# An encoder layer: x read transposed, and the norm's factor moved behind the input projection

## The chip, the cores and the metric

One core of one Trainium2 chip. The metric is the time in microseconds (us) of one execution on the device; the numbers given are medians of several runs.

## The reference

One layer for two request groups that share all weights: a prompt of 2048 tokens and a sample group of 8 x 16 = 128 tokens, 1024 features each. All data are float32.

```
h   = rms_norm(x, norm_g[0])                 # x * rsqrt(mean(x*x) + 1e-6) * g, per token
z   = h @ w_in                               # 1024 -> 3592 columns
qa, ka, va, qb, kb, vb, ob, ib, fb = split(z)
att = chunk-band attention(qa, ka, va)       # 8 heads x 64, own chunk of 64 and 8 before it
hb  = mLSTM(qb, kb, vb, ib, fb)              # 4 heads x 128, matrix memory, blocks of 64
mix = concat(rms_norm(att), sigmoid(ob) * head_norm(hb)) @ w_out
x   = x + rms_norm(mix, norm_g[1])
x   = x + rms_norm(conv_ffn(rms_norm(x, norm_g[2])), norm_g[3])
```

The outputs are x of both groups, the keys and values of the last 512 prompt tokens and of the sample, and the mLSTM and convolution states. Inputs may be laid out in another order before the launch, with no arithmetic.

## The kernel before, in words

Tokens are handled in 17 tiles of 128 rows: tiles 0 to 15 are the prompt, tile 16 (`SAMPLE`) the sample group. The input projection works on two halves, each of three chunks of up to three tiles (`HALVES`): half 0 is 0-2, 3-5, 6-7 and the sample; half 1 is 8-10, 11-13, 14-15.

Each float32 factor of a large product is held as a high and a low part (`hi` rounded to float32r, `lo` the rest), and `mm3` issues three matmuls. So a chunk in SBUF is a tile `hT` [128, 2, 8, 384]: the parts, the 8 blocks of 128 features on the partitions, and the tokens. There are three such buffers (pool phT); a chunk of half 1 takes the buffer of a chunk of half 0 when its last matmul is done.

`norm_tile` (from `norm_steps`) makes one tile of a chunk: it loads the rows `xr` [128 tokens, 1024], ScalarE (ACT) squares them with a running sum, GpSimd (POOL) makes the factor per token by a power of -0.5, VectorE (DVE) multiplies the rows by the factor and by the gain row, and `rows_to_T` transposes the tile in 8 matmuls against the identity on TensorE (PE, tile `hT_pt`) and writes both parts, ACT the high one and DVE the low one.

The projection runs in 14 groups of 256 weight columns for each half, in the order va0, qk0, qk1, va1, qk2, qk3, then qb0, vo0 to qb3, vo3. `load_group` brings a group's weights in two halves through one buffer (`wraw`, tensor `wi_raw`) and splits them a group ahead. In `group_rows` (va, vo) the tokens are the output's partitions, in `group_T` (qk, qb) the features are. Each accumulates 24 matmuls in one of two PSUM buffers (`ps_mm`), evacuates to a stage tile `st` (`evac_scaled`, on ACT, with a constant scale for queries and keys), and stores it to DRAM from ACT's queue.

Attention and mLSTM run beside the projection. They are streams of small units (`att_stream`, `mem_stream`), cut by yields that state their cost on PE and DVE. After each step of a projection group `pump` adds its stated costs to a clock and starts side units only while

```
clock[1] < SHARE * clock[0]        # DVE costs against 0.615 of the PE costs
```

The steps of `load_group` and `norm_steps` are taken along as `ahead` and counted too. Half 0's tiles are made during its first group and half 1's during half 0's last group (vo3, from its third tile on) and half 1's first. `project` multiplies by w_out, two tiles ahead in its loads; when it loads tile 8 it calls `drain`, which runs what is left of the side units without regard to the clock, then closes the pool of the first phase and opens the FFN's (`open_ffn`, `h2_units`).

The final order of instructions on each engine is not that of the program. A scheduler with a model of the machine's time issues on each engine what is ready first, by program order among what is ready; `keep_in_program_order` pins an instruction behind those before it. Loads go out on SP's queue, the stores of the projection on ACT's.

Of the kernel before, what the change touches and what calls it, by code (L numbers as in the profile page):

```python
# [10 lines left out]
F32 = mybir.dt.float32  # L11
F32R = mybir.dt.float32r
# [32 lines left out]
def hymba_step(ctx: ExitStack, tc: tile.TileContext, I: dict, O: dict):  # L45
# [154 lines left out]

    def xr_tag(t):
        return "xr" if 8 <= t < SAMPLE else ("xr", "pth", "ptl")[t % 3]

    def rows_tile(tag, shape, name, dtype=F32):
# [3 lines left out]

    def norm_tile(t, chunk, j, bank):
        tag = xr_tag(t)  # L210
        xr = rows_tile(tag, [P, D], f"xr{t}")
        nc.sync.dma_start(xr, x_src(t))
        if not g0:
            g0.append(norm_row(0))
# [4 lines left out]
        nc.vector.scalar_tensor_tensor(xr, xr, rs, g0[0], op0=ALU.mult, op1=ALU.mult)  # L219
        rows_to_T(xr, chunk, j, f"hT{t}", bank)  # L220

    def evac_scaled(out, in_, scale):
        if scale is None:
            nc.scalar.copy(out, in_)
        else:
            nc.scalar.activation(out, in_, AF.Copy, scale=scale)  # L226

# [14 lines left out]
    def group_T(wh, wl, half, chunks, dsts, scales, name, outs=(None, None)):  # L242
        for c in range(2):
            for ci, tiles in enumerate(HALVES[half]):
                n = len(tiles) * P
                ch = chunks[ci]
                acc = ps_mm(f"{name}_{c}_{ci}")
                for k in range(KT):
                    w = slice(k * 256 + c * P, k * 256 + (c + 1) * P)
                    mm3(acc[:, :n], wh[:, w], wl[:, w], ch[:, 0, k, :n], ch[:, 1, k, :n],  # L250
                        start=(k == 0), stop=(k == KT - 1))
                    if k % 4 == 3:
                        yield n * 12 / 2400, 0.0
                stage = pa.tile([P, 384], F32, tag="st", name=f"{name}_st{c}_{ci}", bufs=2)
                evac_scaled(stage[:, :n], acc[:, :n], scales[c])
                store_T(stage, dsts[c], tiles, outs[c])

    def group_rows(wh, wl, half, chunks, dst, name, width=256, out=None):
        for ci, tiles in enumerate(HALVES[half]):
            for j, t in enumerate(tiles):  # L260
# [9 lines left out]
                stage = pa.tile([P, 384], F32, tag="st", name=f"{name}_st{t}", bufs=2)  # L270
                evac_scaled(stage[:, :256], acc[:, :256], None)
                if width > 256:
                    nc.vector.tensor_copy(gates[:, gate_ix(t), :], acc[:, 256:width])
                s = 4 if t == SAMPLE else t // 4
# [902 lines left out]
    g0 = []  # L1177
    pipes += [Pipe(att_stream()), Pipe(mem_stream())]
    chunks = []
    norms = norm_steps(0)  # L1180
    next(norms)
# [4 lines left out]
    for n_, (half, gi) in enumerate(seq):  # L1186
# [8 lines left out]
        if g[:2] == "va":  # L1195
            it = group_rows(wh, wl, half, chunks, vd[i], nm, 264 if gi == 0 else 256,
                            [O["v_prompt"][i], O["v_sample"][i].unsqueeze(1)])
        elif g[:2] == "qk":
            it = group_T(wh, wl, half, chunks, [qTd[i], kTd[i]], [-(DA ** -0.5), None], nm,
                         [None, [O["k_prompt"][i], O["k_sample"][i]]])  # L1200
        elif g[:2] == "qb":
            it = group_T(wh, wl, half, chunks, [[t_[:, c, :] for t_ in qkbd[i]] for c in range(2)],
                         [None, DH ** -0.5], nm)
        else:
            it = group_rows(wh, wl, half, chunks, vobd[i], nm)
        if half == 0 and gi == 13:
            chunks = []
            norms = norm_steps(1)
        if n_ == len(seq) - 1:
# [4 lines left out]
        for u, (pe, dve) in enumerate(it):  # L1214
# [374 lines left out]
def lay_inputs(inp):  # L1589
# [12 lines left out]
    for i in range(4):  # L1602
# [6 lines left out]
        "x_sample": inp["x_sample"].reshape(P, D),  # L1609
        "norm_g": inp["norm_g"][0],  # L1610
        "g_att": inp["g_att"].reshape(4, P).transpose(1, 0),
        "g_mlstm": inp["g_mlstm"],
# [66 lines left out]
```

## Time and profile before

| | us |
|---|---|
| median of 3 runs | 2814.21 |
| the runs | 2813.83 to 2818.32 |
| the profiled execution | 2812.18 |
| its span | 2810.5 |
| PE busy | 2729.8 (97%) |
| DVE busy | 1871.9 (67%) |
| ACT busy | 1407.5 (50%) |
| POOL busy | 446.2 (16%) |

Busy time is the sum over an engine's instructions, without register, semaphore and DMA-issuing ones. Matmuls overlap each other and the weight loads (PEld), so a busy PE is not PE at its peak. The projection of half 0 runs from about 12 to 531 us, that of half 1 to about 1054, the output projection to about 1330, and the FFN to the end. Names are the program's with numbers left out; L199 is line 199.

### The profile page before, as it was taken

The page shows a single profiled execution, that of the slowest core. Times are in us where ns is not written, and L with a number is a line of the kernel's source. Part 1 is how long each engine was busy: PE and PEld are TensorE (multiplying, and loading weights), DVE is VectorE, ACT ScalarE, POOL GpSimd, SP SyncE. Part 2 cuts the span into 40 slices and gives each one's busy share as a digit, 9 for nine tenths or more (in the row PEclk, how much of TensorE's full clock was granted, in tenths as well). Part 3 has the DMA queues.
Part 4 walks back from the last instruction along what each step waited for, and adds up shares of the span by engine and source line. Part 5 has one row for each costly group of instructions (what it writes and reads, how often), then busy time and mean ns, then how long its engine had stood idle before and what let it go on. Part 6 is the DMA issues. An engine that isn't in the chain of part 4 may idle for free.

```text
span 2810.5 us, 47049 instructions
## 1 busy us (share of the span) xinstructions
PE 2729.8 (97%) x16587; PEld 2550.2 (91%) x16587; DVE 1871.9 (67%) x3442; ACT 1407.5 (50%) x2836; POOL 446.2 (16%) x876
## 2 busy tenths in 40 slices
PE   8899999999999999999999999999999999999998
PEld 7899999998899998878999988799999878999887
DVE  5344455646446678666989886457878854888855
ACT  4345545644356666543545555445555543555533
POOL 1000010211100003244221110011111310222221
PEclk9999999999999999999999999999999999999999
DMA  4544355557555455355645455644544775555585
GB/s 164 170 128 125 111 155 156 177 148 215 164 173 148 141 177 172 106 180 203 199 160 173 162 177 172 218 145 154 157 154 139 266 264 155 171 181 175 188 298 197
DMA packets 313418, 486.04 MB, mean 173 GB/s; under 512 B 55426, under 2 KB 150622, under 8 KB 313054
## 3 DMA queue, kind: packets, MB, share of 16 engines
q1 hardware_dynamic: 274590, 449.21, 50.9%
q10 hardware_dynamic: 38592, 33.83, 3.6%
q8 instruction: 130, 2.13, 0.3%
q14 instruction: 106, 0.87, 0.1%
HBM read 359.36 MB, written 126.70 MB: 173 GB/s over the span
## 4 chain that ended last, share of the span: by engine, by line
PE 51%; DVE 5%; DMA 2%; issue 2%; ACT 1%; POOL 1%; SPq 0%; DVEq 0%; POOLq 0%; ACTq 0%
PE uec L95 5%; PE uec L96 5%; PE uec L97 5%; PE dn L96 4%; PE dn L97 4%; PE dn L95 4%; PE ua L97 3%; PE ua L96 3%; PE ua L95 3%; PE dnm L95 2%; PE dnm L97 2%; PE dnm L96 2%; PE wo L95 1%; PE wo L97 1%; PE wo L96 1%
## 5 line engine op out<-in xcount | busy, mean ns | idle before, releaser
L95 PE MATMUL uec<-B,wuh 128*128 128x384 f32 (+1 forms) x720 | 236.3, 329 | 6.9 <-DVE uu L1492 6.1
L96 PE MATMUL uec<-B,wuh 128*128 128x384 f32 (+1 forms) x720 | 235.2, 327 | 0.0
L97 PE MATMUL uec<-B,wul 128*128 128x384 f32 (+1 forms) x720 | 233.3, 327 | 0.0
L1251 DVE TENSOR_TENSOR gl<-gr,gh 128x768 fp32r<-128x768 f32 (+3 forms) x141 | 118.7, 849 | 163.3 <-ACT gh L1250 163.0
L1250 ACT CAST gh<-gr 128x768 fp32r<-128x768 f32 (+3 forms) x141 | 102.1, 736 | 219.1 <-PE dn L96 194.1
L1250 ACT CAST wuh<-wu 128x512 fp32r<-128x512 f32 x255 | 141.7, 617 | 91.2 <-PE uec L96 87.5
L95 PE MATMUL dn<-wdh,gh 128*128 128x512 f32 x466 | 182.9, 392 | 2.5 <-DVE ug L1403 2.5
L96 PE MATMUL dn<-wdl,gh 128*128 128x512 f32 x466 | 183.9, 395 | 0.0
L97 PE MATMUL dn<-wdh,gl 128*128 128x512 f32 x466 | 168.4, 396 | 0.0
L1251 DVE TENSOR_TENSOR wul<-wu,wuh 128x512 fp32r<-128x512 f32 x255 | 164.3, 683 | 2.8 <-DMA x2d<-mx 2.8
L96 PE MATMUL vo<-wi_l,hT 128*128 128x256 f32 x544 | 155.7, 286 | 0.0
L95 PE MATMUL vo<-wi_h,hT 128*128 128x256 f32 x544 | 154.9, 285 | 0.6 <-DVE mt L199 0.6
L97 PE MATMUL vo<-wi_h,hT 128*128 128x256 f32 x544 | 155.3, 285 | 0.0
L387 DVE CUSTOM_DVE_ANT_0 tmp<-s,nb 128x640 f32<-128x640 f32 (+4 forms) x128 | 94.3, 737 | 77.8 <-PE s L377 74.3
L95 PEld LDWEIGHTS uec<-B,wuh 128*128 128x128 f32 x720 | 135.1, 188 | 11.1 <-DVE uu L1492 8.1
L96 PEld LDWEIGHTS uec<-B,wuh 128*128 128x128 f32 x720 | 135.2, 188 | 0.1
L97 PEld LDWEIGHTS uec<-B,wul 128*128 128x128 f32 x720 | 135.0, 188 | 0.0
L388 ACT ACTIVATE tmp<-tmp,mn 128x640 f32<-128x640 f32 (+4 forms) x128 | 97.6, 762 | 69.9 <-DVE mn L387 65.6
L95 PE MATMUL qk<-hT,wi_h 128*128 128x384 f32 (+1 forms) x384 | 128.6, 335 | 3.5 <-ACT qk_st L226 1.7
L400 DVE TENSOR_TENSOR ptl<-pt,pth 128x640 fp32r<-128x640 f32 (+4 forms) x128 | 93.5, 737 | 55.4 <-ACT pth L399 54.4
L97 PE MATMUL qk<-hT,wi_l 128*128 128x384 f32 (+1 forms) x384 | 128.0, 333 | 0.0
L96 PE MATMUL qk<-hT,wi_h 128*128 128x384 f32 (+1 forms) x384 | 127.8, 333 | 0.0
(409 smaller groups left out, 8886.6 us busy)
## 6 DMA issues: line engine op xcount, KB each, us to landing
wu<-in_w_up SPq DMA_DIRECT2D x220, 256.0 KB, 4.0
wu<-wsd SPq DMA_DIRECT2D x176, 256.0 KB, 3.7
wdr<-in_w_down SPq DMA_DIRECT2D x132, 256.0 KB, 5.4
gr<-gd SPq DMA_DIRECT2D x78, 384.0 KB, 3.9
wi_raw<-in_w_in SPq DMA_DIRECT2D x52, 512.0 KB, 4.3
wsd<-ws SPq DMA_DIRECT2D x88, 256.0 KB, 4.0
gd<-g SPq DMA_DIRECT2D x44, 384.0 KB, 2.7
kraw<-kTd SPq DMA_DIRECT2D x112, 128.0 KB, 3.2
```

Of the source, the lines that this page charges most:

```text
L95: nc.tensor.matmul(out, ah, bh, start=start, stop=False, skip_group_check=onto)
L96: nc.tensor.matmul(out, ah, bl, start=False, stop=False, skip_group_check=onto)
L97: nc.tensor.matmul(out, al, bh, start=False, stop=stop, skip_group_check=onto)
L387: nc.vector.tensor_tensor_reduce(o_, s_, b_, 1.0, 3e38, ALU.add, ALU.min, accum_out=mn)
L388: nc.scalar.activation(tmp[:, :n], tmp[:, :n], AF.Exp, bias=mn, scale=-1.0, accum_out=rsum[:, i % 4, hh:hh + 1])
L400: nc.vector.tensor_tensor(s.ptl[:, sl, qc], ptv, s.pth[:, sl, qc], op=ALU.subtract)
L1250: nc.scalar.copy(h, r)
L1251: nc.vector.tensor_tensor(l, r, h, op=ALU.subtract)
```

## The change

The program gets x a second time, laid out as xT [128, 8, 2176] (feature in block, block, token), and the gain of the first norm as g0T [128, 8].

- A chunk is made from xT by `split_xT`: ACT writes the high part as x times the gain (a factor per partition), DVE the low part. There are no transposes and no multiplication by the factor per token.
- The rows are still loaded (`rows_used`) to be squared and summed; the factor of each tile goes to a column of `rsall`.
- In `group_rows` the evacuation on ACT multiplies by the factor (a scale per partition); the gates likewise on DVE.
- In `group_T`, where tokens are columns, the factor is needed along each row: `norm_factors` writes `rsall` to DRAM and reads it back to all partitions (`rsb`), and the evacuation is a DVE instruction with a constant and `rsb`. For the third chunk of half 0 it is two instructions. The step states 0.56 us of DVE for it.
- `first_half` loads pieces of xT and rows in turn through four row buffers (xr twice, pth, ptl). `second_half` loads a chunk of xT into the place of the low part and splits it there.
- For half 1 xT is first copied, DRAM to DRAM, to `xTd`, in eight DMAs that stand in the program at the fourth group of half 0 (va1, gi == 3).

```diff
+    xTd = dt_([P, KT, SEQ // 2], "xTd")
...
-        ssq = small.tile([P, 1], F32, tag="ssq", name=f"ssq{t}")
-        nc.scalar.activation(chunk[:, 0, :, j * P:(j + 1) * P], xr.rearrange("p (k c) -> p k c", k=KT), AF.Square,
-                             accum_out=ssq)
-        rs = rsqrt_mean(ssq, D, f"n0_{t}")
-        nc.vector.scalar_tensor_tensor(xr, xr, rs, g0[0], op0=ALU.mult, op1=ALU.mult)
-        rows_to_T(xr, chunk, j, f"hT{t}", bank)
...
+        def use():
+            ssq = small.tile([P, 1], F32, tag="ssq", name=f"ssq{t}")
+            nc.scalar.activation(xr, xr, AF.Square, accum_out=ssq)
+            ms = small.tile([P, 1], F32, tag="ms", name=f"n0_{t}_ms")
+            mean_square(ms, ssq, D)
+            nc.gpsimd.tensor_tensor(rsall[:, rs_ix(t):rs_ix(t) + 1], ms, nhalf[:, 0:1], op=ALU.pow)
...
+    def split_xT(ch, c, k, raw):
+        hi, lo, g = ch[:, 0, k, c], ch[:, 1, k, c], g0T[:, k:k + 1]
+        nc.scalar.activation(hi, raw, AF.Copy, scale=g)
+        nc.vector.scalar_tensor_tensor(lo, raw, g, hi, op0=ALU.mult, op1=ALU.subtract)
...
                     if k % 4 == 3:
-                        yield n * 12 / 2400, 0.0
+                        yield n * 12 / 2400, 0.0 if k < 4 else 0.56
...
-                evac_scaled(stage[:, :n], acc[:, :n], scales[c])
+                for cc, factor in rsb[half][ci]:
+                    nc.vector.scalar_tensor_tensor(stage[:, cc], acc[:, cc], scales[c], factor,
+                                                   op0=ALU.mult, op1=ALU.mult)
...
-                evac_scaled(stage[:, :256], acc[:, :256], None)
+                rs = rsall[:, rs_ix(t):rs_ix(t) + 1]
+                nc.scalar.activation(stage[:, :256], acc[:, :256], AF.Copy, scale=rs)
...
-    def norm_steps(half):
-
-        for ci, tiles in enumerate(HALVES[half]):
-            ch = phT.tile([P, 2, KT, 384], F32R, tag="hT", name=f"hT{half}_{ci}", bufs=3)
-            chunks.append(ch)
-            for j, t in enumerate(tiles):
-                norm_tile(t, ch, j, ps_big)
-                yield 0.9, 2.5
+    def norm_factors(half):
+        a, m = 9 * half, 9 - half
+        nc.sync.dma_start(rsd[a:a + m].rearrange("j p -> p j"), rsall[:, a:a + m])
+        wide = lambda j, n: rsd[j:j + n].rearrange("j p -> (j p)").unsqueeze(0).broadcast_to([P, n * P])
+        r = const.tile([P, D], F32, tag="grow", name=f"rsb{half}")
+        nc.sync.dma_start(r, wide(a, 8))
...
+    def first_half():
...
+        part(0, 0, [0], list(range(KT)))
+        for ks in ([0, 1, 2], [3, 4, 5], [6, 7]):
+            part(0, 1, [1, 2], ks)
+        for t in range(3):
+            factor(t)
+        for ci in (1, 2):
+            for i, k in enumerate(range(0, KT, 2)):
+                part(ci, 0, HALVES[0][ci], [k, k + 1])
+                if i:
+                    factor(HALVES[0][ci][i - 1])
...
+        for n in (1, 4, 3, 3, 2, 3, 3, 2):
+            go(n)
+            if not items and not loaded:
+                norm_factors(0)
+            yield 0.0, 2.2
+
+    def second_half():
+
+        for ci, tiles in enumerate(HALVES[1]):
+            ch = new_chunk(1, ci)
+            n = len(tiles) * P
+            raw = ch[:, 1].bitcast(F32)
+            nc.sync.dma_start(raw[:, :, :n], xTd[:, :, (tiles[0] - 8) * P:(tiles[0] - 8) * P + n])
+            use = rows_used(tiles[0], "xr")
+            yield 0.0, 0.0
+            use()
+            use = rows_used(tiles[1], "xr")
+            for k in range(4):
+                split_xT(ch, slice(0, n), k, raw[:, k, :n])
+            yield 0.0, 2.2
...
+            if half == 0 and gi == 3 and u < KT:
+                nc.sync.dma_start(xTd[:, u], I["xT"][:, u, SEQ // 2:SEQ])
```

More of the change, by code (lines that the diff above doesn't have):

```diff
@@ L222, in evac_scaled @@
[L222 to L226, printed above, removed]
+        def use():
[4 more added lines that the diff above has]
+            nc.gpsimd.tensor_tensor(rsall[:, rs_ix(t):rs_ix(t) + 1], ms, nhalf[:, 0:1], op=ALU.pow)
@@ new lines, in new_chunk, with part, load, factor @@
+    def new_chunk(half, ci):
+        chunks.append(phT.tile([P, 2, KT, 384], F32R, tag="hT", name=f"hT{half}_{ci}", bufs=3))
+        return chunks[-1]
+    def first_half():
+        tags = ["xr", "pth", "ptl", "xr"]
+        items = []
+        def part(ci, j, tiles, ks):
+            def load(tag):
+                ch = chunks[ci] if ci < len(chunks) else new_chunk(0, ci)
+                return staged(ch, j * P, tiles, ks, tag, f"xT{ci}_{j}_{ks[0]}")
+            items.append(load)
+        def factor(t):
+            items.append(lambda tag: rows_used(t, tag))
+        part(0, 0, [0], list(range(KT)))
[8 more added lines that the diff above has]
+                    factor(HALVES[0][ci][i - 1])
+        loaded = deque()
+        def go(n):
+            for _ in range(n):
+                while items and len(loaded) < 3:
+                    loaded.append(items.pop(0)(tags[0]))
+                    tags.append(tags.pop(0))
+                loaded.popleft()()
+        for n in (1, 4, 3, 3, 2, 3, 3, 2):
[3 more added lines that the diff above has]
+            yield 0.0, 2.2
```

56 lines of the change are left out of this document (44 added, 12 removed).

## The prediction

> **What bounds the kernel now.** I read the page's first two parts, then the busy time by windows over the first 48 us, the chain of events there in the timeline, the groups by tile, and the waits of the tensor engine.
>
> ```profile
> span 2810.5 us, 47049 instructions
> PE 2729.8 (97%) x16587; PEld 2550.2 (91%) x16587; DVE 1871.9 (67%) x3442; ACT 1407.5 (50%) x2836; POOL 446.2 (16%) x876
> ```
>
> The tensor engine (PE) is busy 97% of the span, so an instruction taken off its queue is time saved, unless it then waits for something else. All that the change touches lies in two short stretches, the start and the change of halves, and in the evacuations of the projection between them.
>
> ```profile
> 0.00:10.00 10.00, 1.83 (x8) 1.57 (x8) 2.97 (x9) 3.97 (x6) 2.64 (x17) 1.00 0.72 268
> 10.00:20.00 10.00, 7.87 (x45) 7.43 (x45) 7.67 (x9) 7.40 (x13) 2.55 (x8) 1.00 0.71 237
> 20.00:30.00 10.00, 9.87 (x85) 9.69 (x84) 8.82 (x12) 7.11 (x13) 2.94 (x5) 1.00 0.62 215
> 30.00:40.00 10.00, 10.00 (x87) 10.00 (x86) 6.67 (x10) 5.01 (x10) 0.74 (x2) 1.00 0.67 193
> sum 48.40, PE 35.78 PEld 34.45 DVE 28.22 ACT 26.66 POOL 9.60; mean PE 7.16 PEld 6.89 DVE 5.64 ACT 5.33 POOL 1.92
> ```
>
> Columns are PE, PEld, DVE, ACT, POOL, then clock, DMA share and GB/s. Up to 48.4 us, where the second weight group begins, PE idles 48.4 - 35.8 = 12.6 us, most of it in the first 15 us. From 20 to 40 us it is full: group va0 is then PE-bound, and the transposes of x are part of what fills it.
>
> ```profile
> 1.70 0.43 SPq L1155 DMA_DIRECT2D wi_raw<-in_w_in  x1
> 3.89 0.66 SPq L1227 DMA_DIRECT2D bgate<-in_b_gate  x1
> 6.71 0.36 SPq L485 DMA_DIRECT2D hgm<-in_g_mlstm  x1
> 10.38 0.33 SPq L1155 DMA_DIRECT2D wi_raw<-in_w_in  x1
> 14.52 1.17 ACT L1161 CAST wi_h<-wi_raw 128x528 fp32r<-128x528 f32 x2 [0.76 <-DMA wi_raw<-in_w_in]
> 18.11 0.37 PE L95 MATMUL va<-wi_h,hT 128*128 128x264 f32 x1
> 45.89 1.03 PE L67 MATMUL hT_pt<-ident,xr 128*128 128x128 f32 x8
> 48.37 0.34 PE L95 MATMUL qk<-hT,wi_h 128*128 128x384 f32 x1
> L643 DVE SCALAR_TENSOR_TENSOR mvo<-mvo,hgm x32: 408/426/623, 276.5 to 1140.4; 128x256 f32<-128x256 f32 x32
> ```
>
> Two facts carry the forecast. First, the second half of group va0's weights goes through the one wraw buffer: its load is issued at 10.38, after the first half is split, and lands at 14.52; only then can tile 0 be finished (18.11). Second, SP's order is not the program's: the gain hgm, first used at 276.5, is loaded at 6.71, and bgate, written in the program after all of va0, at 3.89. A DMA that needs nothing and has its buffer free goes out as soon as SP is free.
>
> **The change, part by part.** (1) *Transposes gone.* 17 tiles lose 8 transposes each, 1.03 us of PE by the row at 45.89: 9.3 us for half 0, 8 x 1.03 = 8.2 us for half 1. PE's waits for their input go too:
>
> ```profile
> PE hT_pt L67 <- DVE xr L219: 1.3, 2, 1.1
> ```
>
> That is the wait in 480 to 600 us, so half 1 gains 8.2 + 1.3 = 9.5 us. What could be late next there is the chunk: it is loaded into its own slot, free after the third tile of vo3 in half 0, and wanted after the ninth:
>
> ```profile
> 502.34 0.37 ACT L224 COPY vo_st<-vo 128x256 f32<-128x256 f32 x1 [1.01 <-PE vo L97]
> 537.19 0.36 ACT L224 COPY va_st<-va 128x256 f32<-128x256 f32 x1
> 500.00:550.00 50.00, 47.62 (x405) 46.79 (x403) 32.99 (x63) 33.11 (x74) 13.44 (x31) 1.00 0.61 185
> ```
>
> From 502 to the first va tile (evacuated at 537, so begun near 532) there are 30 us for a load of 1.6 MB and 16 splits of about half a microsecond on each of two engines; that is covered. But half 1 now reads x twice (4.2 MB transposed, 4.2 MB as rows, each 8 tiles of 512 KB), where the DMA engines are already 0.61 busy. The extra 4.2 MB take about 14 us of them in some 50 us; I charge 2 us for later loads of the side work (bounds 0 and 5).
>
> (2) *The copy of x's second half.* Eight DMAs of 512 KB, DRAM to DRAM, stand in the program at the fourth group, but need nothing and write a buffer nobody holds. Like hgm they will be issued right after the first loads, between about 5 and 10 us, in front of the second half of the weights. The nearest row for such a burst is the copies of the relative bias, eight of 383.5 KB:
>
> ```profile
> relrow<-ext SPq DMA_DIRECT2D x8, 383.5 KB, 8.4
> L298 SPq DMA_DIRECT2D relrow<-ext x8: 470/596/1928, 80.9 to 88.4; - x8
> 90.00:95.00 5.00, 1.09 (x7) 0.77 (x5) 0.00 (x0) 0.26 (x1) 0.00 (x0) 1.00 1.08 291
> ACT pk L570 <- DMA relrow<-ext: 9.1, 1, 9.1
> PE pkTp L67 <- ACT pk L573: 4.8, 1, 4.8
> ```
>
> They fill the DMA engines at 291 GB/s, ACT stood 9.1 us behind them and PE 4.8. At that rate 4.2 MB take 14.4 us. The weights' second half then lands near 28 instead of 14.5, and tile 0 is finished near 29 instead of 18.
>
> (3) *The start as a whole.* It becomes a matter of bytes. Before the last chunk of half 0 is whole, these come in: xT 4.7 MB (9 tiles), rows of 8 tiles 4.2, two weight groups 2.1, the copies 4.2. Rates for whole and for short pieces, each a count of bytes, mean rate and share of the 16 DMA engines (8 to 18 us, then 300 to 330):
>
> ```profile
> DMA packets 1242, 2.98 MB, mean 298 GB/s; under 512 B 408, under 2 KB 536, under 8 KB 1242
> q1 hardware_dynamic: 1242, 2.98, 84.1%
> ...
> DMA packets 3497, 3.32 MB, mean 111 GB/s; under 512 B 876, under 2 KB 2924, under 8 KB 3495
> q1 hardware_dynamic: 2343, 2.31, 26.7%
> q10 hardware_dynamic: 1152, 0.98, 9.7%
> ```
>
> 298/0.841 = 354 GB/s for mostly 4 KB rows, 111/0.364 = 305 for pieces around 1 KB; xT comes in pieces of 512 to 1536 B. So 6.3/354 + 4.7/305 + 14.4 us = 17.8 + 15.4 + 14.4 = 47.6 us, plus 4 us before the first byte and from the last byte to its landing (an estimate: the weight load of 10.38 took 4.1 us to land, of which 540 KB at 354 GB/s are 1.5), 1.1 us of splits, and the rest of PE's work on the last chunk (two tiles and a bit, 24 matmuls a tile, at 87 in 10 us by the row at 30 us 2.8 us each: 6.6). That is 59.3, against 48.4: +11. If all bytes went at 354 and the copies too, 15.2/354 = 43 us, and the end is 54.6: +6. I take +10, nearer the first, since copies and short pieces have rows of their own. Half 0's transposes are in this difference. The Trainium skill, "DMA: Bandwidth & Descriptors", section Specifications, puts the least piece for line rate at 512 B; by it xT would cost 13.3 us and not 15.4, and the start +9. The two windows here speak for the lower rate, though they also hold other transfers.
>
> (4) *Evacuations from ACT to DVE.* 96 of them, and 16 extra pieces for the sample tile.
>
> ```profile
> L199 DVE TENSOR_TENSOR mt<-mT_pt,mt 128x512 fp32r<-128x512 f32 x16 | 10.8, 684 | 1.7 <-ACT mt L198 1.6
> L695 DVE SCALAR_TENSOR_TENSOR cst<-cst,dec,ma 128x129 f32<-128x129 f32 x64 | 21.9, 342 | 8.5 <-PE ma L694 8.4
> L219 DVE SCALAR_TENSOR_TENSOR xr<-xr,n_rs,norm_row 128x1024 f32<-128x1024 f32 x17 | 21.8, 1286 | 16.5 <-POOL n_rs L84 11.3 <-DMA norm_row<-in_norm_g 5.2
> L199 DVE TENSOR_TENSOR hT<-hT_pt,hT 128x1024 fp32r<-128x1024 f32 x17 | 20.7, 1217 | 3.5 <-ACT hT L198 3.5
> 150.00:200.00 50.00, 50.00 (x338) 49.77 (x337) 23.22 (x47) 23.96 (x53) 0.58 (x4) 1.00 0.39 116
> ```
>
> Between 342 ns (129 columns) and 684 (512) a 384-column one is about 550: 96 x 0.55 + 16 x 0.34 = 58 us more on DVE. The row norm and the transposed split go (21.8 + 20.7 = 42.5); the new splits are 56 pieces of 128 to 384 columns at 0.35 to 0.55, some 28. DVE gains 44 us over 1050, about 2 in 50 where it is 23 busy: no bound. PE has two accumulators, and at 338 matmuls in 50 us (row at 150) the 24 of one accumulation give 3.5 us of cover; DVE must be later than that to cost anything. I charge 1 us (0 to 3). The first such evacuation also waits for the factors of all nine tiles, written to DRAM and read back as 512 KB: some 8 us after row 16 is squared, by SP's queue, with two va tiles and two accumulations (2 x 2.8 + 2 x 3.5 = 12.6 us) as cover. What stands behind that wait on SP is the next group's weights, wanted a group later.
>
> (5) *The planner.* It starts side work only while its sum of DVE costs is under 0.615 of its sum of PE costs. The change adds 96 x 0.56 = 53.8 to the one, takes 17 x 2.5 - 14 x 2.2 = 11.7 off, and takes 17 x 0.9 x 0.615 = 9.4 off the allowance: 51.5 less for attention and memory. Going through the code's costs unit by unit, the pipes are empty in both cases late in half 0, which absorbs most of it; the side work before finishes exactly at the drain (tile 8 of the output projection), and afterwards 14 steps of 18.2 us PE and 18.2 us DVE (planner's units) are left for it.
>
> ```profile
> 1190.00:1200.00 10.00, 1.60 (x10) 1.24 (x10) 1.55 (x2) 1.29 (x2) 1.00 0.01 2
> 1200.00:1210.00 10.00, 0.00 (x0) 0.00 (x0) 0.00 (x0) 0.00 (x0) 1.00 0.52 170
> 1280.00:1290.00 10.00, 0.60 (x4) 0.49 (x4) 1.96 (x3) 0.58 (x1) 1.00 0.86 263
> 1329.11 0.34 PE L95 MATMUL ua<-B,wuh 128*128 128x384 f32 x1
> ```
>
> The first two rows are tile pt: the last attention transposes of before end at 1200, which bears out the count. The third is h2T_pt: the FFN's inputs are ready by 1290, 39 us ahead of its first matmul, so a later drain does not delay the FFN. Projection matmuls that are ready can fill PE in the drain. I charge 3 us, between 0 and 9 (half of the 18.2 idle).
>
> Sum: +10 - 9.5 + 2 + 1 + 3 = +6.5 us. The profiled execution took 2812.2 us (span 2810.5 and 1.7 around it), so 2818.7 there; the median of the runs shown is 2.0 us above it: **2821 us**. A measurement of this kernel can tell 0.2%, 5.6 us, from no change.
>
> **Rivals.** *A, faster: the copies do not hurt the start* (they go out at the fourth group, a little before 150 us, where the row at 150 shows a DMA share of 0.39, or the weights' second half gets past them). It decides at the point where that load is issued: before or after the copies. The start is then 17.8 + 15.4 + 4 + 7.7 = 44.9, or 42 by PE's work alone (9 tiles x 2.8 from 17 us on, where the weights are whole); with some waits for the four row buffers I take 46, -2.5. Sum: -2.5 - 9.5 + 1 + 1 + 3 = -7, 2807. For it: the place in the program. Against: hgm and bgate. 0.25.
>
> *B, a tie:* bytes at the best rate (+6) and the drain wholly filled: 6 - 9.5 + 2 + 1 + 0 = -0.5, 2814. 0.2, with the lower part of the forecast's own spread.
>
> *C, slower still: the drain is bare.* Attention alone in a chain, PE idle half of it (9), DVE late for accumulators (3) and loads of half 1 late (5): 10 - 9.5 + 5 + 3 + 9 = 17.5, 2832. It decides if PE shows idle stretches between 1190 and 1230 beyond those of before. 0.12.
>
> **How the numbers follow.** The forecast has 0.43. Forecast and C give slower 0.55, B the same 0.2, A faster 0.25. The range goes from a little below A, 2804, to a little above C, 2834; the likeliest case alone has 2815 to 2828.
>
> **What would show it.** Right: eight xTd issues on SP before 12 us; the second wi_raw landing after 24; the first qk matmul near 58; no hT_pt; vo3 of half 0 to va0 of half 1 shorter by 8 to 9; a few us of attention after the point where the output projection reaches tile 7. Wrong: the copies late, or the first qk matmul before 48; or PE waiting in the qk and qb groups for DVE more than a few us in all.

## The result, and the profile after

| | median, us | runs | lowest to highest |
|---|---|---|---|
| before | 2814.8 | 6 | 2813.1 to 2818.3 |
| after | 2885.4 | 6 | 2880.9 to 2893.0 |

The change makes the kernel slower: the ratio is 1.025 (95% interval 1.0235 to 1.0268), 71 us where 6.5 were forecast. The profiled execution took 2889.7 us. Its page begins so:

```profile
span 2888.0 us, 47051 instructions
PE 2751.5 (95%) x16451; PEld 2558.4 (89%) x16451; DVE 1900.8 (66%) x3576; ACT 1389.6 (48%) x2779; POOL 448.9 (16%) x876
```

136 matmuls fewer (17 tiles of 8 transposes), and PE is busy 21.7 us longer and idle 136.5 us instead of 80.7. Where that lies is told by the start of a few groups, read from the timelines of both profiled executions (us from the span's start, for after the difference from before; qk0_0 is group qk0 of half 0 and qk3_1 group qk3 of half 1, wo the output projection's first matmul, wo8 its sample tile, wo9 its first tile of half 1, ua the FFN's first matmul, end the end of the last one):

```
            qk0_0   qk1_0   qk2_0   vo3_0   qk3_1   qb0_1     wo0     wo8     wo9      ua     end
before       48.4    82.2   155.9   489.0   721.2   757.4  1055.5  1208.1  1228.9  1329.1  2802.9
after       +11.8   +21.8   +30.0   +28.5   +19.5   +26.6   +24.0   +20.5   +68.1   +68.2   +77.5
```

Three steps carry nearly all of it: +30.0 up to the third qk group, -9.0 from vo3 of half 0 to qk3 of half 1 (the next groups take 7.1 of these back and give 6.1 again), and +47.6 between two tiles of the output projection. The last 9.3 arise in the FFN; this profiled execution is itself 4 us above the median.

**The start.** The timeline has the forecast's chain, the copies first (SPq is the DMA queue of SP):

```profile
5.96 2.73 SPq L1323 DMA_DIRECT2D xTd<-in_xT  x3
...
16.45 0.33 SPq L1186 DMA_DIRECT2D wi_raw<-in_w_in  x1
...
26.70 1.17 ACT L1192 CAST wi_h<-wi_raw 128x528 fp32r<-128x528 f32 x2 [1.32 <-DMA wi_raw<-in_w_in]
...
27.39 0.81 PE L95 MATMUL va<-wi_h,hT 128*128 128x264 f32 x2 [8.71 <-ACT wi_h L1192]
...
60.22 0.34 PE L95 MATMUL qk<-hT,wi_h 128*128 128x384 f32 x1
```

The weights' second half is split at 26.7 instead of 14.5, and the first qk matmul is at 60.2. But the start is not over there. The busy time by windows (PE, PEld, DVE, ACT, POOL, then clock, DMA share, GB/s) shows the next hole, and the waits between 55 and 80 us what made it:

```profile
50.00:60.00 10.00, 9.24 (x71) 8.74 (x72) 2.40 (x7) 4.26 (x8) 1.48 (x4) 1.00 0.67 204
60.00:70.00 10.00, 8.78 (x52) 8.41 (x50) 3.07 (x15) 2.86 (x6) 0.74 (x2) 1.00 0.26 37
70.00:80.00 10.00, 3.90 (x13) 3.62 (x12) 1.17 (x6) 1.53 (x4) 0.40 (x2) 0.66 0.63 187
```

```profile
57.19 0.38 SPq L1201 DMA_DIRECT2D rsd<-rsall  x1
71.41 0.32 SPq L1204 DMA_DIRECT2D rsb<-rsd  x1
```

```profile
SPq L1204 <- DMA rsd<-rsall: 13.8, 1, 13.8
DVE qk_st L284 <- DMA rsb<-rsd: 6.7, 1, 6.7
PE qk L95 <- DVE qk_st L284: 6.1, 1, 6.1
```

The factors of nine tiles are 4.6 KB, but they go to DRAM in 1152 pieces of four bytes, and SP stood 13.8 us until they had landed. From 60 to 70 us the DMA engines moved 37 GB/s: everything else that SP had to send, weights and the relative bias, stood behind that wait. The write also held up what another queue had sent. A store that ACT's queue issued beside it, at 57.3 us, landed only with it, after 13.9 us (first row); the median of all stores of its kind is 2.9 (second row):

```profile
vd<-va_st ACTq DMA_DIRECT2D x2, 128.0 KB, 13.9
vd<-va_st ACTq DMA_DIRECT2D x32, 128.0 KB, 2.9
```

PE filled both accumulators and stopped. The Trainium skill, "DMA: Bandwidth & Descriptors", section Specifications, says that pieces under 512 B are done as read-modify-write. That bears on this write, against which the prediction did not weigh it; the rows show that the write is slow, not by what mechanism.

PE goes on waiting for evacuations behind that chain. Over the whole kernel its waits for them are these, with the 6.1 us of above among the first five; three more of the five lie between 118 and 132 us and one at 104. Before, PE waited 2.8 us for ACT's evacuations:

```profile
PE qk L95 <- DVE qk_st L284: 12.4, 5, 6.1
PE qb L95 <- DVE qk_st L284: 3.5, 1, 3.5
```

Third, all squares of x rows, half 1's too, are done by 160 us:

```profile
L225 ACT ACTIVATE xr<-xr x17: 1045/1058/1062, 17.6 to 159.7; 128x1024 f32<-128x1024 f32 x17
```

Since the square no longer writes into the chunk, the chunk's buffer no longer holds half 1's row loads back, and 4.2 MB that the prediction had put into half 1 join the start.

**The drain.** Attention's last matmuls, and what PE does until the output projection goes on (timeline, engines mixed):

```profile
1247.61 0.80 SPq L1003 DMA_DIRECT2D mr<-mixd  x2
...
1270.79 0.69 PE L67 MATMUL ao<-ident,attT 128*128 128x128 f32 x2 [0.91 <-DVE attT L450]
...
1272.24 0.55 SPq L465 DMA_DIRECT2D mixd<-attst  x1
...
1273.55 8.70 SPq L1092 DMA_DIRECT2D x2r<-x2d  x3
1279.49 1.06 ACT L1100 ACTIVATE sq<-x2r 128x1024 f32<-128x1024 f32 x1 [9.21 <-DMA x2r<-x2d]
...
1281.58 1.28 DVE L1104 SCALAR_TENSOR_TENSOR x2r<-x2r,n_rs,g 128x1024 f32<-128x1024 f32 x1 [9.28 <-POOL n_rs L84]
...
1281.81 0.61 ACT L1008 ACTIVATE mt<-mr 128x512 fp32r<-128x512 f32 x1
...
1282.92 1.12 PE L1112 MATMUL h2T_pt<-ident,x2r 128*128 128x128 f32 x4 [11.44 <-DVE x2r L1104]
...
1294.51 1.97 PE L67 MATMUL mT_pt<-ident,mr 128*128 128x128 f32 x8 [4.62 <-DVE mr L1010]
...
1296.98 0.78 PE L95 MATMUL wo<-wo,mt 128*128 128x512 f32 x1
```

The sample tile's matmuls ended at 1245; attention then ran alone until 1271, with PE busy 18.8 of 26.3 us. Only then is the attention's memory given up and the FFN's opened (line 1062 onwards), and its chain begins: load, square, factor, scaling, transposes. The rows of the next projection tiles (`mr`) are loaded from 1247.6 on, but their norm (1281.81) and transposes stand behind that chain on ACT's and PE's queues, and so wo9 starts 25.5 us after attention's last matmul. Before, that distance was 21.3 us, and the sample tile's 11.4 us of matmuls covered part of it. In the whole gap from wo8 to wo9 PE was idle 5.0 us before and is idle 25.5 now. The clock falls with it (PE's busy time is the second figure, the clock the one before the DMA share):

```profile
1260.00:1270.00 10.00, 7.51 (x38) 6.59 (x36) 3.86 (x7) 3.68 (x9) 0.00 (x0) 0.73 0.00 0
1270.00:1280.00 10.00, 0.69 (x2) 0.29 (x2) 1.21 (x3) 0.79 (x2) 0.00 (x0) 0.50 0.63 183
1280.00:1290.00 10.00, 5.03 (x20) 3.86 (x20) 6.32 (x6) 5.47 (x13) 8.31 (x13) 0.50 0.33 106
```

The Trainium skill, "TensorE: Matmul & The Clock Gate", section What's actually happening, gives the idle array half its clock after about 3.4 us without work. The granted 0.50 in the hole of 11.44 us and behind it agrees; but the clock was at 0.50 from 1261.1 to 1264.5 and again from 1267.9 on, while attention ran alone and no single idle time of PE was over 1.2 us, and that the rule does not cover.

### The profile page after: what moved, and what is told of

The parts are those of the page before. It is cut to its first block, busy times and chain, and to the rows that moved or that the text cites. A ratio compares the mean times of both kernels' runs of the same rounds, so it can differ in the third digit from the quotient of the medians.

```text
span 2888.0 us, 47051 instructions
## 1 busy us (share of the span) xinstructions
PE 2751.5 (95%) x16451; PEld 2558.4 (89%) x16451; DVE 1900.8 (66%) x3576; ACT 1389.6 (48%) x2779; POOL 448.9 (16%) x876
## 4 chain that ended last, share of the span: by engine, by line
PE 49%; DVE 4%; DMA 2%; issue 2%; ACT 1%; POOL 1%; SPq 0%; DVEq 0%; POOLq 0%; ACTq 0%
PE uec L95 6%; PE uec L96 5%; PE uec L97 5%; PE dn L95 3%; PE dn L96 3%; PE dn L97 3%; PE ua L97 3%; PE ua L95 3%; PE ua L96 3%; PE dnm L95 2%; PE dnm L97 2%; PE dnm L96 2%; PE ub L95 1%; PE ub L96 1%; PE ub L97 1%
## 5 line engine op out<-in xcount | busy, mean ns | idle before, releaser
L95 PE MATMUL qb<-hT,wi_h 128*128 128x384 f32 (+1 forms) x384 | 128.1, 334 | 3.5 <-DVE qk_st L284 3.5
```

Of the source, the lines that this page charges most:

```text
L95: nc.tensor.matmul(out, ah, bh, start=start, stop=False, skip_group_check=onto)
```

## The experiments

Eighteen kernels were run; the table has all of them, with the difference of group starts from before (us, profiled executions, as above) and the ratio of times. Prices in the text are by the ratios where they are of whole runs, since each run has its own runs of before beside it. A single start says little below some 5 us: e11, whose time is that of before, stands up to 4.7 us late, though by at most 1.6 more from one column to the next.

```
                                                 qk0_0  qk2_0  qk3_1    wo0    wo8    wo9    end   ratio  (95%)
after                                            +11.8  +30.0  +19.5  +24.0  +20.5  +68.1  +77.5  1.0251 (1.0235-1.0268)
e1   after, planner's cost 0                     +11.0  +33.8  +24.1  +31.2  +42.5  +42.9  +46.6  1.0179 (1.0164-1.0194)
e2   after, copies held                           +4.6  +15.5   +1.4   +4.7   +1.6  +46.7  +52.3  1.0194 (1.0170-1.0217)
e3   after, factors as rows, late                +11.9  +11.9  +56.2  +32.3  +31.5  +78.8  +83.2  1.0306 (1.0288-1.0323)
e4   e1+e2+e3, half 1's row loads held            +4.1   +1.6  +61.4  +55.3  +81.2  +92.6  +97.4  1.0337 (1.0319-1.0355)
e8   e1+e2, half 0's factors alone as rows        +3.7  +13.8   +8.6  +10.1  +22.4  +23.3  +28.1  1.0092 (1.0074-1.0111)
g    e8, half 1's rows spread over half 0         +3.5   +0.9   -3.3   -3.0   +9.0   +9.7  +11.4  1.0040 (1.0025-1.0056)
e5   before, planner's cost 0.56                  +0.5   -4.1   -3.1   +5.5   +3.2  +43.4  +42.8  1.0147 (1.0132-1.0162)
e7   before, the copies added                    +11.4  +14.2  +10.6  +10.1  +10.2   +9.8   +7.7  1.0007 (0.9995-1.0020)
e9   before, 96 evacuations on DVE                +0.8   -0.5   +9.1   +9.7  +29.3  +40.5  +37.1  1.0102 (1.0072-1.0131)
e10  before, half 0's 48 on DVE                   -0.1   -0.2   +6.9   +7.8  +26.6  +37.2  +34.0  1.0111 (1.0090-1.0132)
e11  before, six on DVE (qb0 of half 0)           +0.3   +0.9   +2.3   +3.9   +4.7   +4.2   +3.0  1.0004 (0.9994-1.0014)
e12  before, six on DVE (qk1 of half 0)           -0.3   +0.5   +4.8   +3.3  +22.6  +33.5  +36.8  1.0144 (1.0129-1.0160)
f    half 0 as before, half 1 as after            +3.3  +12.9   +7.1  +13.1  +25.3  +26.1  +31.4  1.0098 (1.0083-1.0114)
h    f, half 1's rows spread over half 0          +1.9   +6.5  +14.3  +18.3  +30.8  +31.8  +37.7  1.0127 (1.0100-1.0154)
h2   h, planner's threshold 0.63                  +2.4   +6.5  +13.8   +6.6  +36.2  +35.0  +38.7  1.0126 (1.0099-1.0153)
k1   half 0 as before, half 1 scaled ahead        +1.9   +5.7  +21.1  +29.5  +28.7  +28.4  +32.7  1.0160 (1.0135-1.0185)
k2   g, half 1 scaled ahead of the split          +6.4   +2.9  +14.4  +25.3  +35.8  +36.0  +41.6  1.0153 (1.0135-1.0171)
k3   k1, loads placed again                       +2.2   +2.5   -2.4   +2.9   +2.5   +1.8   +5.9  1.0038 (1.0025-1.0050)
```

**e1, the planner's cost.**

```diff
-                        yield n * 12 / 2400, 0.0 if k < 4 else 0.56
+                        yield n * 12 / 2400, 0.0
```

> The changed kernel with the planner's cost of a scaled evacuation set from 0.56 to 0, nothing else. Theory (the planner holds attention back until the drain): counted through the code's costs, the drain then finds 0 us of side work left and not 18.2; the gap from tile 8 to tile 9 of the output projection falls from 68.5 us to about 21 (before: 20.8), while the attention that moves forward takes its PE time there (up to 18 us). Total 28 to 48 us less: 2837 to 2857. Rival (attention is late because the start is late and DVE is fuller, whatever the costs say): the drain stays, total 2875 to 2890.

2862.4 us. The gap from wo8 to wo9 is 21.2 us again, as the planner theory has it, but 22 of the 47 us come back as attention done earlier (wo8 at +42.5). Net it is 0.72% or 20 us, less than the range given. So the drain is the planner's, and its price in the whole kernel is smaller than the gap.

**e2, the copies held**: `tc.keep_in_program_order(...)` around the eight copies.

> The changed kernel with the eight copies of x's second half held at their place in the program (fourth group); nothing else. Theory (the copies stand in front of the weights and of half 0's x): the second half of va0's weights is issued near 10 us and not at 16.45, the first qk matmul comes 8 to 11 us earlier than 60.2, total 2874 to 2878. Rival (the start is bound by what else must come in, rows and transposed x, or the 4-byte factor write ends last all the same): the first qk matmul moves by less than 4 us, total 2881 to 2887.

```profile
L1323 SPq DMA_DIRECT2D xTd<-in_xT x8: 512/612/3242, 119.6 to 170.4; - x8
```

```profile
14.12 0.33 SPq L1186 DMA_DIRECT2D wi_raw<-in_w_in  x1
```

2865.6 us, by the ratios 16 less, more than either theory gave. The second half of the weights goes out at 14.1 instead of 16.5, and not near 10; the first qk matmul comes 7.2 us earlier, a little less than the theory's 8 to 11; and the gain grows to 14.5 at qk2. So the theory's order is right and its total too low: the copies cost as much again behind the first qk matmul as up to it.

**e3, the factors as rows**: turned by one transpose on PE, copied to SBUF, and written after the last va tile.

```diff
-        nc.sync.dma_start(rsd[a:a + m].rearrange("j p -> p j"), rsall[:, a:a + m])
+        nc.tensor.transpose(pt[:m, :P], rsall[:, a:a + m], ident)
+        nc.vector.tensor_copy(rsT[:m, :P], pt[:m, :P])
+        nc.sync.dma_start(rsd[a:a + m], rsT[:m, :P])
```

> The changed kernel with the factors turned on PE and written to DRAM as rows of 512 B, after the last va tile, in place of the 4-byte pieces; nothing else. Theory (the write of 1152 four-byte pieces, 13.8 us in the trace, stands in the path and on SP): the write lands within 3 us, PE's stop between 70 and 76 us goes, the second qk group starts 8 to 15 us earlier than 104.0, total 2870 to 2878. Rival (PE waits there for bytes, the next weights and the relative bias, all the same): second qk group within 4 us of 104, total 2881 to 2887.

In half 0 the theory holds, for form and later place of the write together: SP's wait is 2.9 us instead of 13.8 (first row), and qk1 and qk2 start 14.7 and 18.1 us earlier than in after.

```profile
SPq L1208 <- DMA rsd<-rsT: 2.9, 1, 2.9
```

```profile
L1205 SPq DMA_DIRECT2D rsd<-rsT x2: 296/302/307, 61.7 to 669.9; - x2
```

The total is a miss, 2896.6 us. The second row says why: half 1's factors, written at 162 us in after, now go out at 669.9, and the first qk group of half 1, begun at 575, stands until they are there; side work done meanwhile gives back part.

**e4, all edits, and half 1's row loads held.**

> All three edits together, and the loads of the eight row tiles of half 1 held at their place in the program (the trace has them issued from 56 to 153 us, among the first half's loads). Theory (start, factor write and drain are separate terms and add): 2810 to 2832, with qk2 of half 0 starting within 12 us of before (155.9) and the gap at tile 8 near 21. Rival (one of them only uncovers another wait, or the larger part lies in DVE work moved from ACT): above 2845.

2906.9 us, far above the range: half 1's rows and factors again come late (qk3_1 at +61.4). What it shows is the start: qk2_0 is 1.6 us behind before.

**e8 and g: half 1's factors left as in the change; then its rows spread out.**

> The changed kernel with planner's cost 0, the copies held at their place, and the factors of half 0 alone turned on PE and written as rows; half 1's factors and row loads stay as the change has them. Theory (the three terms are separate; the loss of the earlier run with all edits came from half 1's factors reaching the queue late): qk2 of half 0 starts 0 to 8 us after before's 155.9, the stretch from there to the output projection is 6 to 10 us shorter than before's, total 2804 to 2822. Rival (side work piles up whatever the start does): the output projection's tile 8 starts more than 25 us late, total above 2830.

2841.3 us, above the range: at qk2 13.8 are left, the rows of half 1, and the output projection loses 12 (wo0 to wo8).

```diff
+            if half == 0 and 4 <= gi < 8 and u in (1, 6):
+                late_row = rows_used(2 * gi + (u == 6), "xr")
+            if half == 0 and 4 <= gi < 8 and u in (5, 10):
+                late_row()
```

> The run with three edits (planner's cost 0, copies held, half 0's factors as rows) and one more: half 1's row loads and squares spread over the groups qk2 to vo0 of half 0, its factors written in qb1. Theory (the early rows cost the start 11 us, the difference at qk2 between the two runs that have them early and late): qk2 of half 0 starts 0 to 5 us after before's 155.9, total 2827 to 2834. Rival (the loads cost the same where they are put): 2838 to 2845.

2824.9 us, a little below the range. The start is before's within 0.9 us, 12.9 us are gone: that is the price of the early rows beside held copies and short factor writes. 59 of the 71 us are recovered in g, the best version of the change. What is left is not at the start: up to wo0 g is 3.0 us ahead of before, from there to wo8 it loses 12.

**e5 and e7: two parts of the change alone, in the kernel before.**

> The kernel before with one edit: the planner is told 0.56 us of DVE for each evacuation of the qk and qb groups, as in the change; no instruction is added or taken. Theory (the drain comes from the planner's sums alone): counted through the code's costs, 15.4 us of PE and 15.9 us of DVE side work are left for tile 8 of the output projection; the gap from tile 8 to 9 grows from 20.8 us to 55 to 70, some 20 of it is won back ahead of it, total 2832 to 2842. Rival (the late start and the fuller DVE made the drain of the changed kernel): 2808 to 2820.

2856.4 us, above the range. Not one instruction is added, only their order is another, and 41 us are lost, at the place expected:

```profile
1246.15 0.69 PE L67 MATMUL ao<-ident,attT 128*128 128x128 f32 x2 [0.91 <-DVE attT L419]
1258.31 1.12 PE L1081 MATMUL h2T_pt<-ident,x2r 128*128 128x128 f32 x4 [11.47 <-DVE x2r L1073]
```

It is the hole of after, 11.47 us, and wo9 starts 25.5 us after attention's last matmul here too. That 20 us would be won back ahead of it was wrong: wo8 is 3.2 us late, although attention's matmuls are missing there.

> The kernel before with the eight copies of x's second half added where the change has them, free to be issued early, and never read. Theory (the copies alone cost the start what holding them back gave): they are issued before the second half of va0's weights, the first qk matmul comes 5 to 12 us later than 48.4, total 2820 to 2832. Rival (they hurt only beside the doubled reads of x): less than 4 us later, 2809 to 2817.

```profile
L1224 SPq DMA_DIRECT2D xTd<-in_xT x8: 490/496/640, 7.6 to 16.0; - x8
```

The copies go out as in after and the start loses 11.4 us at the first qk matmul, 14.2 at qk2, as expected. Over the whole run the profiled execution shows 8 to 10 of them, the times none that is certain (interval -0.05 to +0.20%), so what is lost at the start need not reach the end.

**f, h and h2: half 1 alone changed.** Half 0 with rows, transposes and ACT as before.

> Half 0 as before (rows, transposes on PE, evacuations on ACT); half 1 as in the change (transposed x, split directly, factors at the evacuations), with the copies held at the fourth group and the planner's cost 0. Theory (half 1's eight tiles of transposes are the gain that the change has): 2801 to 2810. Rival (row loads of half 1 come early and take the start's bandwidth, and the evacuations on DVE take the rest): 2811 to 2822.

> Half 0 as before, half 1 as in the change, copies held, cost 0, and half 1's rows spread over half 0's groups qk2 to vo0. Theory (the 12 us that this split lost up to qk2 of half 0 were the early rows and copies): 2828 to 2836. Rival (they were lost to something else): 2840 to 2846.

> As the run before it, with the planner's threshold raised from 0.615 to 0.63. Theory (the 12 us that every run with cost 0 loses in the output projection are attention left over from half 1, since the transposes that went no longer count as PE time; 336 attention matmuls stand there and not 316): the output projection's first eight tiles take 153 us again and not 165, total 2812 to 2824. Rival (its length does not hang on the planner): within 4 us of the run before it.

2843.2, 2850.4 and 2850.6 us; none met the range of its theory. f loses 12.9 us up to qk2 of half 0; h, with half 1's rows spread, wins half of that back and loses 12 us in vo1 of half 0. There half 1's factors are written in four-byte pieces at 341.2, SP sends the next weights half a microsecond behind, and ACT waits for these until 357:

```profile
ACT wi_h L1199 <- DMA wi_raw<-in_w_in: 14.0, 1, 14.0
```

h2 does move attention, but the wrong way: 182.1 us for the first eight tiles of the projection instead of 165.1, and the same total.

**e9 and e10: the evacuations on DVE.** The kernel before with

```diff
-                evac_scaled(stage[:, :n], acc[:, :n], scales[c])
+                nc.vector.scalar_tensor_tensor(stage[:, :n], acc[:, :n], -2.0 * (scales[c] or 1.0),
+                                               nhalf[:, 0:1].broadcast_to([P, n]), op0=ALU.mult, op1=ALU.mult)
```

> The kernel before with the 96 evacuations of the qk and qb groups moved from ACT to DVE (a product with two constants in place of the factors), nothing else. Theory (DVE has room, two accumulators cover it): each takes about 0.55 us on DVE, total 2812 to 2819. Rival (DVE serves attention and memory in the same stretches, so these come later and the wait moves to the output projection): the output projection starts 8 us or more late, total above 2824.

> The kernel before with the evacuations of the qk and qb groups on DVE in half 0 only (48 of the 96). The run with all 96 moved was 28 us slower; its profile loses 6.5 us up to the end of half 0 and the rest later, most of it in the output projection. Theory (the loss comes from half 1's, which push attention into the output projection): 2814 to 2820, output projection's tiles 0 to 7 within 3 us of 152.5. Rival (work pushed out of half 0 piles up to the end as well): half of the loss, 2824 to 2830.

2841.7 and 2845.5 us. In e9 the rival's signs came (the output projection 9.7 us late, the total above 2824), in e10 neither range was met: all 96 cost 29 us, and half 0's 48 cost as much (31), though e10 is 0.2 us ahead at qk2 and 3.3 behind at vo3 of half 0: most of it comes in the output projection (18.8 from wo0 to wo8) and behind it (10.6), in code that e10 doesn't touch. The time that the moved instructions take on DVE, all of it in half 0, does not explain that.

**e11 and e12: six evacuations.** What differs in every run that loses there is the order of PE's instructions, which is fixed when the kernel is built. Counted in the traces, attention's matmuls (s, pt, ot, ao; 1744 in all) that start ahead of the output projection, its length from wo0 to wo8, and the gap from wo8 to wo9:

```
            ahead of wo0   wo0-wo8   wo8-wo9
before          1428        152.5      20.8
e7, e11         1428        152.7, 153.3   20.5, 20.4
k3              1428        152.1      20.2
e1, e8, g       1408        163.8, 164.9, 164.5   21.2, 21.7, 21.6
e9              1398        172.2      32.0
e10, e12        1389        171.4, 171.8   31.5, 31.8
e5              1385        150.2      61.1
after           1358        149.0      68.4
```

Moving one group of six evacuations shifts the order or doesn't, by which group it is.

> The kernel before with the six evacuations of one group, qb0 of half 0, on DVE. In the order in which PE's instructions are laid down at the build, 1428 attention matmuls stand ahead of the output projection, as before. Theory (the loss of the runs with evacuations on DVE comes from the order of the instructions, not from DVE's time): 2811 to 2817. Rival (DVE's time): 3.3 us of it at most, 2811 to 2818; this run alone doesn't tell them apart, it is the control for the next.

> The same with another single group, qk1 of half 0: six evacuations, 3.3 us of DVE. Here 1389 attention matmuls stand ahead of the output projection, as in the run with half 0's 48 evacuations moved. Theory (order): as slow as that run, 2835 to 2846. Rival (DVE's time): 2811 to 2818.

2814.1 us for e11, no change (interval -0.06 to +0.14%), and 2850.4 for e12, a little above the range and 40 us slower, each with 3.3 us of work moved between engines. So it is not the amount of DVE's work; and e5, in which the order alone differs, shows that the order can cost as much. A run with e12's evacuations and the order of before was not made. The windows from wo0 to wo8 and on to wo9, of before and of e12:

```profile
1055.50:1208.10 152.60, 148.75 (x870) 127.73 (x869) 113.81 (x222) 85.24 (x218) 45.41 (x67) 1.00 0.44 136
1208.10:1228.90 20.80, 15.86 (x73) 12.49 (x71) 10.93 (x13) 9.07 (x20) 9.81 (x14) 0.92 0.52 153
```

```profile
1058.80:1230.60 171.80, 159.65 (x926) 135.62 (x925) 123.39 (x250) 96.03 (x244) 47.14 (x75) 0.99 0.43 133
1230.60:1262.40 31.80, 19.33 (x84) 15.30 (x84) 16.73 (x17) 9.77 (x20) 12.61 (x15) 0.72 0.50 154
```

56 more matmuls stand in the projection, 37 of them attention's and the others the mLSTM's; they add 10.9 us of busy PE and 8.3 of idle (12.15 instead of 3.85). And since attention then ends at 1236.9, in the middle of the sample tile (1230.6 to 1242.5), less of that tile is left to cover the FFN's chain: PE is idle 12.5 us in the gap instead of 4.9. In the mixers' groups ahead, which lost those matmuls, e12 saves only 2.4 us (qb0_1 to wo0: 295.8 for 298.2): PE is busy 5.0 us less there and idle 2.7 more. Why it saves so little is not shown.

**k1, k2, k3: the removed transposes by themselves.** Half 1's x is scaled by gain and factor ahead of the split, so evacuations and order stay as before (k1, k3; k2 does it on top of g).

> Half 0 as before; half 1 from transposed x with the whole norm, gain and factor, multiplied in ahead of the split, so that all evacuations stay as before; rows of half 1 and their factors spread over half 0's groups, copies held at the fourth group. It differs from the kernel before by half 1's 64 transposes on PE, 8.2 us and 1.3 of waits, and by the loads. Theory (half 1's transposes are worth what was charged): 2802 to 2808. Rival (the loads in half 0 or late chunks eat it): 2812 to 2822.

> The changed kernel with cost 0, copies held, half 0's factors as rows, half 1's rows spread over half 0, and in half 1 the factor multiplied in ahead of the split, so that half 1's evacuations go back to ACT. Theory (of the 11.6 us that the best changed version so far still loses, all comes from half 1's evacuations on DVE): 2803 to 2812. Rival (half 0's evacuations cost as much): 2816 to 2822.

2859.7 and 2856.1 us, k1's loss whole and 28 of k2's 42 us up to qb2 of half 0: there the factors were written tile by tile, and SP stood for each (k1 is 32 us late at qb2 of half 0).

> The version with half 1's whole norm in the split, once more, with its loads placed so that the SP queue does not stand: factors written in one piece at qb1, their read held until qb3, copies spread over qk2 to vo0. Its attention order is that of before (1428). Theory (the removed 64 transposes of half 1 are worth 8 to 9 us, as the stretch from vo3 to qk0 of half 1 of the earlier version shows, and its loss was the queue's): 2803 to 2810. Rival (loads and splits take it back): 2811 to 2825.

2820.6 us, 0.38% slower than before, as the rival has it. From vo3 of half 0 to qk0 of half 1 it gains 8.7 us, near what the transposes were charged with, though 22 matmuls of side work have left that stretch too. It gives back more than that later, the largest part, 4.6 us, from qb0_1 to wo0:

```profile
755.70:1058.50 302.80, 298.91 (x2276) 294.03 (x2274) 183.74 (x416) 184.09 (x441) 19.20 (x60) 1.00 0.54 161
```

```profile
757.40:1055.50 298.10, 297.05 (x2274) 292.82 (x2273) 181.97 (x414) 182.23 (x438) 18.22 (x58) 1.00 0.55 162
```

The same matmuls, to two, take 302.8 us (first row, k3) and not 298.1 (before): 2.8 us more idle, 1.9 more busy. Why is open, and no version tried beats the kernel before.

## Why the prediction was wrong

The sign was right, with 0.55 on slower; the time is outside the range by 51 us, and of what was lost only the first 11.8 us came about as worked out. Of the signs that the prediction named, the second half of the weights behind 24 us (26.7), the first qk matmul near 58 (60.2) and the missing hT_pt came. Others did not: the last of the eight copies goes out at 18.9 us and not before 12, vo3 of half 0 to va0 of half 1 is 0.4 us shorter and not 8 to 9, and attention runs alone for 26.3 us where a few were expected. One of its signs of being wrong came: PE waits 15.9 us in all for DVE in the qk and qb groups. By its steps:

1. *Transposes.* Right in size, not in place: in the changed kernel the stretch that held them, vo3 of half 0 to qk0 of half 1, is only 1.6 us shorter, since 64 transposes are gone and 20 more matmuls of side work stand there. Up to qk3 of half 1, with 60 matmuls fewer in all, it is 9.0 us for 9.5 charged. That they stay gained was taken for granted, and k3 shows that they don't.
2. *The copies.* Right in kind: issued from 5.96 us on, seven of the eight ahead of the weights' second half. Their price by themselves is 11.4 us at the first qk matmul and 14.2 at qk2 (e7), though e7's whole time is at most 0.2% longer.
3. *The start as bytes.* Right as far as it went: the first qk matmul at 60.2, +11.8 for +10. The estimate by the 512 B of the Trainium skill ("DMA: Bandwidth & Descriptors", section Specifications), +9, was the lower of the two and further off; the trace does not test it, since other loads share that stretch. The step failed in its end: the start was taken to be over at the first qk matmul, and 18 us more came behind it.
4. *Evacuations and factors.* Two failures. The "some 8 us after row 16 is squared" for the factor chain left out in what pieces it is written: the write held SP for 13.8 us, and e3, which changes its form and its place, sets its price at 18 us at qk2. And "What stands behind that wait on SP is the next group's weights, wanted a group later" named the right queue and took it for harmless. An evacuation takes 0.55 us on DVE, as forecast. That all 96 cost PE no more than 1 us is not shown: e11 moves only six, for no change, PE's waits for them are 15.9 us in the changed kernel with the factor chain's 6.1 among them, and e9 starts the output projection 9.7 us late. And moving instructions between engines changed the order in which PE's instructions are built; the runs in which it changed lose 29 to 40 us in the kernel before (e9, e10, e12). The prediction had no such term. Whether the part of it in the changed kernel adds to the planner's is not separated: with the planner's cost at 0, e8 and g still lose 12 us in the projection, with 1408 matmuls ahead of it.
5. *The planner.* The count of what is left for the drain was right in kind (150 attention matmuls stand behind wo8), and rival C named the place. Its size was near too: 18.2 us were counted, and those of the 150 that run alone keep PE busy 18.8. The price failed: 3 us, 9 at most, against 47.6 at the place, 20 of the total in the changed kernel (e1) and 41 in the kernel before (e5). The failing sentence is "Projection matmuls that are ready can fill PE in the drain". None are once the sample tile is done: attention runs alone for 26.3 us, the FFN's opening waits for its end, and the next tile's norm and transposes stand behind that opening on ACT and PE, another 25.5 us in which PE is busy 7.5.
6. *Loads in half 1*, 2 us: the rows were not loaded there but at the start, where they cost 12.9 us (e8 against g). The prediction saw that SP's order is not the program's, and applied it to the copies alone.

The start's three prices, 14.5, 18.1 and 12.9, come to 45.5 and the start lost 30.0, so they overlap; e4 and g show that together they are all of it. From the milestones, +30.0 at the start, -1.5 on the way, -9.0 to qk3 of half 1, +1.0 to wo8, +47.6 at the drain, +0.1 to the FFN and +9.3 in it make the 77.5 of the profiled execution. The FFN's part ranges from -3.4 (e9) to +9.3 (after) over the runs, with no edit in it; its cause is open.

## What to carry to other kernels

When a wait or a dependency goes, ask of every instruction that it held back, DMAs above all, when it will be issued now, and estimate a small DMA's cost by its pieces and by what is on the way beside it and behind it, not by its bytes. Where side work fills an engine, count at the known edges (here the output projection) how much of it stands ahead, before and after; with a shift of 39 attention matmuls of 1744 went a loss of 40 us. And a drain is priced by the chain that starts only when it ends, not by the work left in it.

## What was not expected of the hardware

A write of 4.6 KB from SBUF to DRAM took 13.8 us as 1152 pieces of four bytes, and SP's wait was 2.9 us with the same factors as nine rows of 512 B. While that write was under way the DMA engines moved 37 GB/s between 60 and 70 us. SP issued nothing behind it, but that is not all: a store of 128 KB that ACT's queue had issued landed with the write, after 13.9 us for a median of 2.9, and in h weights that SP did issue behind such a write kept ACT waiting 14.0 us.
